# Two mixers of a fused two-block model: recurrence in one pass, squares summed on TensorE, conditioning steps at fixed places

## The chip, the cores and the metric

One core of a Trainium2 chip runs the whole program. The metric is the device time of one execution in microseconds (us). TensorE is written PE, VectorE DVE, ScalarE ACT, GpSimd POOL and SyncE SP, as in the profile.

## What is computed

Two model blocks run one after the other on 256 tokens of width 1024. The change touches the first block alone, which has two layers, and 16 tokens are put ahead of the 256, so that T = 272. A layer is a mixer and a feed-forward part. Cut to the mixer:

```python
hn = rms_norm(h, norm_mix_g[l])
q, k, v, xr, gate = jnp.split(hn @ w_in[l], splits, axis=-1)
o_attn = rms_norm(diff_attention(q, k, v, lam), subln_g[l]) * (1.0 - lam_init)
# recurrent branch: conv of width 4 over xr gives xc; r and i are sigmoids of small products of xc
log_a = LRU_C * r * log_sigmoid(lru_L);  a = exp(log_a)
u = sqrt(max(-expm1(2 * log_a), 0)) * i * xc          # the root is replaced by 1 at token 0
h_t = a_t * h_(t-1) + u_t                             # along the tokens
o_rec = rms_norm(h_t * gelu(gate), rec_norm_g[l])
h = h + concatenate([o_attn, o_rec]) @ w_out[l]       # 512 + 512 rows of w_out
```

Beside this the program computes `silu(c) @ w_ada` (the conditioning), which only the second block reads.

## The kernel before

**Layout.** Activations of the first block are held with channels on partitions: `h` is 8 chunks of 128 channels by 272 tokens. Each fp32 product is three fp32r products (`mm3`, lines 364 to 366): high part of the weight with high and with low part of the input, and low part with high. `weights()` hands out the next weight block, loads run three blocks ahead on SP's queue, and each block is split by ACT (`whi`, line 340) and DVE (`wlo`, line 342).

**A mixer** (`first_mixer`). After the projections for k, q and v, `first_attend` (a generator) does the attention of two tiles of 128 tokens; each of its first four steps is a head, its fifth normalises and transposes the tile's output into `mh` and `ml`, chunks 0 to 3. Between the heads the loop traces `taps(c)` (projection and convolution of chunk c) and `gate(c)` (projection, gelu, the two small products of line 749 and four ACT functions). Then come the root over all four chunks (line 776), `recurrence(c)` for each chunk (lines 758 to 762, scan on 761), the sum of its squares over channels, a reciprocal root per token (`rstd_row` and `rsqrt`, lines 399 to 407, then the broadcast by PE on line 451 and the copy `RR`), and the multiplication and split into `mh` and `ml`, chunks 4 to 7 (lines 783 to 785).

**The output projection** runs in two halves, first over chunks 0 to 3 of `mh` (attention), then over 4 to 7 (recurrence). Each half has four weight blocks b of two output chunks c, 96 products in all. Each result is added to `h` from PSUM (line 799).

**PSUM.** `acc` has 3 banks, `st` 1, and the mixer has `sc` 2, `pt` 1, `po` 1. `pt` is shared by the transposes of the heads and the products of the gates.

**Conditioning.** `ada_steps` is a generator of 32 steps, 16 for each mixer. A step loads a tile of 512 KB (`wada`, five buffers; the first five loads on SP's queue, the others on POOL's) and does four matmuls of 32 columns (line 487, eight passes in the trace) into an `acc` bank that is held over 16 steps. The 16th also copies the bank (line 492) and transposes it (line 496).

**Order.** Within an engine the order is fixed when the program is built: a scheduler takes, of the instructions that it believes to be ready, the one that was traced first. `high_priority` counts a block as traced earlier. `issue_after(x)` makes instructions of a block queue behind x on the engine of x, without a wait. Each engine then takes its instructions strictly in that order.

Of the kernel before, what the change touches and what calls it, by code (L numbers as in the profile page):

```python
# [7 lines left out]
F32 = mybir.dt.float32  # L8
# [24 lines left out]
HP = 400  # L33
ADA = ((4, 4, 4, 2), (4, 4, 4, 0))
SUMS = ((0, 4), (0, 5)) + tuple((1, p) for p in range(6))
# [247 lines left out]
class Net:  # L283
# [83 lines left out]

    def gemm(self, w, m, xs, cols, n, ps=None):

        if ps is None:  # L370
            ps = self.psum("acc")[:, :n]
        m = slice(128 * m, 128 * m + 128)
        for k, (wk, xk) in enumerate(zip(w, xs, strict=True)):
            self.mm3(ps, [t[:, m] for t in wk], [t[:, cols] for t in xk], k == 0, k == len(w) - 1)
        return ps
# [57 lines left out]

    def rstd_row(self, pool, ss, tiles, width, mul, name, eps=EPS, extra=False):


        nc = self.nc
        st = self.psum("st")
        big = [(i, t) for i, t in enumerate(tiles)]
        for i, (t0, tn) in big:  # L440
            a0 = t0 if tn == 128 else 0
            nc.tensor.matmul(st[:, i:i + 1], ss[:, a0:a0 + 128], self.ones[:, 0:1], start=True, stop=True)
        n = len(tiles) + extra
        if extra:
            for j in range(4):
                nc.tensor.matmul(st[32 * j:32 * j + 32, n - 1:n], ss[:, 0:32], self.ones[:, 0:1], start=True, stop=True,
                                 tile_position=(0, 32 * j))
        y, v = self.rsqrt(st[:, :n], (128, n), mul, eps, "ry", pool)
        bc = self.psum("st")
        for i, (t0, tn) in big:  # L450
            nc.tensor.matmul(bc[:, t0:t0 + tn], y[0:tn, i:i + 1].to_broadcast([tn, 128]), self.idt[0:tn, 0:tn],
                             start=True, stop=True)
# [21 lines left out]
    def ada_steps(self):  # L474
# [3 lines left out]
        for b in range(2):  # L478
# [14 lines left out]
            cols = [j for j in range(4) if 4 * b + j not in (4, 5, 10, 11)]  # L493
            p2 = self.psum("st")
            for m in range(4):
# [124 lines left out]
    def first_mixer(self, l, mp, fp):  # L620
# [102 lines left out]

        xc, gts = [], []
        tr = mp.tile([128, 4, T], F32, name="tr")
        th = mp.tile([128, 4, T], F32, name="th")

        def taps(c):
            xr = mp.tile([128, T], F32, tag="xr", name="xr", bufs=2)
            nc.vector.tensor_tensor(xr, self.gemm(self.weights(), 0, xs, al, T), R, op=ALU.mult)  # L730
            x = mp.tile([128, T], F32, name=f"xc{c}")
            cw = self.par("conv_w", l, 0, 16)
            nc.scalar.activation(x, xr, AF.Identity, scale=cw[:, 12 + c:13 + c], bias=self.par("conv_b", l, c))
            for i in range(3):
                s = 3 - i
                nc.vector.scalar_tensor_tensor(x[:, s:], xr[:, :T - s], cw[:, 4 * i + c:4 * i + c + 1], x[:, s:],
                                               op0=ALU.mult, op1=ALU.add)
            xc.append(x)

        def gate(c):  # L740
            x = xc[c]
            gt = mp.tile([128, T], F32, name=f"gt{c}")
# [10 lines left out]
            nc.vector.scalar_tensor_tensor(x, ti, 1.0, x, op0=ALU.add, op1=ALU.mult)  # L753

        rs = mp.tile([128, T], F32, name="rs")

        def recurrence(c):
            nc.vector.scalar_tensor_tensor(th[:, c], tr[:, c], 1.0, th[:, c], op0=ALU.add, op1=ALU.mult)
            nc.vector.memset(th[:, c, 0:1], 1.0)
            nc.vector.tensor_tensor(xc[c], xc[c], th[:, c], op=ALU.mult)  # L760
            nc.vector.tensor_tensor_scan(xc[c], tr[:, c], xc[c], 0.0, op0=ALU.mult, op1=ALU.add)
            nc.vector.tensor_tensor(xc[c], xc[c], gts[c], op=ALU.mult)
            self.sumsq_add(rs, self.sp, xc[c], c == 0, T)

# [5 lines left out]
        for i in range(2):  # L770
            for u, _ in enumerate(att(i)):
                if u < 4:
                    f, c = next(parts)
                    f(c)
        nc.vector.tensor_scalar(th, th, 0.0, None, op0=ALU.max)
        nc.scalar.activation(th, th, AF.Sqrt)
        for c in range(4):
            recurrence(c)
        RR, _, _ = self.rstd_row(mp, rs, tiles, T, 1.0 / (512 * 16), "RR")
        g4 = mp.tile([128, 4], F32, name="g4")  # L780
        nc.vector.tensor_scalar(g4, self.par("rec_norm_g", l, 0, 4), 0.25, None, op0=ALU.mult)
        for c in range(4):
            nc.vector.tensor_tensor(xc[c], xc[c], RR, op=ALU.mult)
            nc.scalar.activation(mh[:, 4 + c], xc[c], AF.Copy, scale=g4[:, c:c + 1])
            nc.vector.scalar_tensor_tensor(ml[:, 4 + c], xc[c], g4[:, c:c + 1], mh[:, 4 + c].bitcast(F32),
                                           op0=ALU.mult, op1=ALU.subtract)


        oc = slice(0, T) if l + 1 < DEPTH else slice(META, T)
        on = oc.stop - oc.start  # L790
        g = self.par("norm_ffn_g", l, 0, 8)
        for half in (0, 1):
            ys = [(mh[:, 4 * half + k], ml[:, 4 * half + k]) for k in range(4)]
            for b in range(4):
                w = self.weights()
                for m in range(2):
                    c = 2 * b + m
                    ps = self.gemm(w, m, ys, oc, on)
                    nc.vector.tensor_tensor(self.h[:, c, oc], self.h[:, c, oc], ps, op=ALU.add)
                    if half == 1:  # L800
                        self.cols = oc
                        self.first_pre(c, g)
                if half == 0:
                    self.ada_step(ADA[l][b])

    def first_attend(self, mp, l, i, qk, vn, aq, nlam, sub, mh, ml):
# [10 lines left out]
        for h in units:  # L817
# [39 lines left out]
            if i < 2:  # L857
                o = po[:, 128 * h:128 * h + 128]
                nc.tensor.matmul(o, am, vn[2][0:16, h], start=True, stop=False)
                for j in range(nt):  # L860
                    nc.tensor.matmul(o, a[:, 128 * j:128 * j + 128], vn[j][:, h], start=False, stop=j == nt - 1)
# [24 lines left out]
        nc.scalar.activation(mh[:, 0:4, d], src, AF.Copy, scale=sub)  # L886
        nc.vector.scalar_tensor_tensor(ml[:, 0:4, d], src, sub, mh[:, 0:4, d].bitcast(F32), op0=ALU.mult, op1=ALU.subtract)
        yield
# [713 lines left out]
```

## Time and profile before

| what | value |
|---|---|
| time, median of 3 runs | 1690.88 us (1690.41 to 1691.0) |
| the profiled execution, its own time | 1690.12 us |
| its span, first to last instruction | 1688.3 us |
| mean granted clock of PE | 0.987 of full speed |
| PE / weight loads / DVE / ACT / POOL busy | 97% / 83% / 75% / 50% / 4% |
| mixer 0 | to about 159 us |
| mixer 1 | about 364 to 513 us |

A line of the timeline has the start, the length, the engine, the line of the kernel, the operation, output<-inputs, the count and, in brackets, the idle time before it and who ended it. PE lengths overlap: matmuls are pipelined, and two starts tell more than one length. A granted clock of 1.00 is 2.4 GHz and 0.50 is 1.2 GHz; a value between them is a mean over both.

### The profile page before, as it was taken

Reading aid. Unit: us, or ns where it says so; the run is one execution under the profiler, and the core shown is the slowest. Engines: PE = TensorE matmul, PEld = TensorE weight load, DVE = VectorE, ACT = ScalarE, POOL = GpSimd, SP = SyncE. Lnnn points to the kernel's source line nnn. Section 1 sums busy time; section 2 is a strip of 40 time slices with the busy share of each in tenths; the row PEclk is TensorE's granted clock in tenths of the full one; section 3 lists DMA queues with packets and bytes.
Section 4 is the critical chain, followed back from the end, with each engine's and each line's share of the span. In section 5 each row is a group of like instructions: output and inputs, shape, how many; then the busy total and the mean of one; then the engine's idle time right before and its main releaser. Section 6 shows DMA issues by size and latency. Waiting matters only on the chain.

```text
span 1688.3 us, 27336 instructions
## 1 busy us (share of the span) xinstructions
PE 1638.9 (97%) x10336; PEld 1397.0 (83%) x10336; DVE 1258.5 (75%) x2706; ACT 846.6 (50%) x1607; POOL 69.5 (4%) x143
## 2 busy tenths in 40 slices
PE   7999999999989999999999999999999999979998
PEld 7868999998869999997667987788787786679997
DVE  7678897675878776664566887898986978587777
ACT  5575544354747544534465543232332757665554
POOL 0001000000010000000010000001110000000000
PEclk9999999999989999999999999999999999989999
DMA  7546665464356656523223254556672231245663
GB/s 260 163 149 240 200 211 174 154 193 149 102 175 192 182 183 188 181 76 100 64 69 111 78 162 137 187 162 200 220 242 87 90 98 40 65 131 184 184 186 112
DMA packets 71852, 256.77 MB, mean 152 GB/s; under 512 B 8585, under 2 KB 8601, under 8 KB 71721
## 3 DMA queue, kind: packets, MB, share of 16 engines
q1 hardware_dynamic: 56904, 203.58, 38.1%
q0 software_dynamic: 14672, 51.45, 9.5%
q8 instruction: 81, 1.33, 0.3%
q14 instruction: 51, 0.41, 0.1%
q10 hardware_dynamic: 144, 0.00, 0.0%
HBM read 253.92 MB, written 1.07 MB: 151 GB/s over the span
## 4 chain that ended last, share of the span: by engine, by line
PE 79%; issue 10%; DVE 5%; ACT 3%; DMA 2%; POOL 0%; DVEq 0%; ACTq 0%; SPq 0%; POOLq 0%
PE acc L364 14%; PE acc L365 14%; PE acc L366 14%; PE up L365 6%; PE up L364 6%; PE up L366 6%; PE y L364 2%; PE y L366 2%; PE y L365 2%; PE po L1390 2%; PE pt L1384 2%; DVE wlo L342 1%; ACT whi L340 1%; PE sc L1379 1%; DMA wada<-wada 1%
## 5 line engine op out<-in xcount | busy, mean ns | idle before, releaser
L340 ACT ACTIVATE whi<-raw 128x1024 fp32r<-128x1024 f32 (+2 forms) x436 | 397.2, 924 | 540.3 <-PE acc L365 245.3
L342 DVE TENSOR_TENSOR wlo<-raw,whi 128x1024 fp32r<-128x1024 f32 (+2 forms) x436 | 456.6, 1055 | 209.5 <-ACT whi L340 204.2
L364 PE MATMUL acc<-hi,whi 128*128 128x272 f32 (+1 forms) x848 | 248.7, 294 | 8.1 <-ACT hi L575 7.4
L366 PE MATMUL acc<-hi,wlo 128*128 128x272 f32 (+1 forms) x848 | 246.4, 291 | 0.8 <-DVE wlo L342 0.8
L365 PE MATMUL acc<-lo,whi 128*128 128x272 f32 (+1 forms) x848 | 246.6, 291 | 0.0
L364 PEld LDWEIGHTS acc<-hi,whi 128*128 128x128 f32 x848 | 161.9, 191 | 15.7 <-ACT hi L575 7.7
L364 PE MATMUL acc<-op,whi 128*128 128x256 f32 (+1 forms) x528 | 165.3, 315 | 0.0
L365 PE MATMUL acc<-op,whi 128*128 128x256 f32 (+1 forms) x528 | 164.1, 312 | 0.1
L366 PE MATMUL acc<-op,wlo 128*128 128x256 f32 (+1 forms) x528 | 163.4, 310 | 0.0
L365 PEld LDWEIGHTS acc<-lo,whi 128*128 128x128 f32 x848 | 161.8, 191 | 1.7 <-DVE lo L576 0.3
L366 PEld LDWEIGHTS acc<-hi,wlo 128*128 128x128 f32 x848 | 161.8, 191 | 1.2 <-DVE wlo L342 0.8
L364 PE MATMUL acc<-whi,op 128*128 128x512 f32 (+1 forms) x424 | 151.1, 357 | 0.1
L365 PE MATMUL acc<-wlo,op 128*128 128x512 f32 (+1 forms) x424 | 150.8, 356 | 0.0
L365 PE MATMUL up<-op,whi 128*128 128x512 f32 (+1 forms) x384 | 146.6, 382 | 0.0
L364 PE MATMUL up<-op,whi 128*128 128x512 f32 (+1 forms) x384 | 145.6, 381 | 0.8 <-ACT whi L340 0.7
L366 PE MATMUL up<-op,wlo 128*128 128x512 f32 (+1 forms) x384 | 145.4, 380 | 0.0
L366 PEld LDWEIGHTS acc<-op,wlo 128*128 128x128 f32 x528 | 100.7, 191 | 7.9 <-issue 3.0
L531 DVE SCALAR_TENSOR_TENSOR asum<-wadb,csp,asum 128x1024 f32<-128x1024 f32 x84 | 107.1, 1276 | 0.0
L364 PEld LDWEIGHTS acc<-op,whi 128*128 128x128 f32 x528 | 99.6, 189 | 7.9 <-issue 1.6
L365 PEld LDWEIGHTS acc<-op,whi 128*128 128x128 f32 x528 | 99.6, 189 | 7.0 <-issue 1.5
L364 PEld LDWEIGHTS acc<-whi,op 128*128 128x128 f32 x424 | 80.0, 189 | 13.2 <-issue 0.7
L365 PEld LDWEIGHTS acc<-wlo,op 128*128 128x128 f32 x424 | 79.8, 188 | 12.8 <-issue 1.8
(443 smaller groups left out, 3380.7 us busy)
## 6 DMA issues: line engine op xcount, KB each, us to landing
raw<-wts SPq DMA_DIRECT2D x362, 512.0 KB, 3.8
wadb<-wadb POOLq DMA_DIRECT2D x64, 512.0 KB, 4.0
wada<-wada POOLq DMA_DIRECT2D x27, 512.0 KB, 6.3
raw<-wts SPq DMA_DIRECT2D x8, 384.0 KB, 3.1
B<-brow SPq DMA_DIRECT2D x6, 512.0 KB
wada<-wada SPq DMA_DIRECT2D x5, 512.0 KB, 6.3
nb<-nbias POOLq DMA_DIRECT2D x16, 128.0 KB, 2.4
h<-xm SPq DMA_DIRECT2D x4, 272.0 KB, 4.1
```

The costliest lines, as they stand in the source:

```text
L340: nc.scalar.activation(hi[:, cs], raw[:, cs], AF.Copy)
L342: nc.vector.tensor_tensor(lo[:, cs], raw[:, cs], hi[:, cs].bitcast(F32), op=ALU.subtract)
L364: mm(out, a[0], b[0], start=start, stop=False)
L365: mm(out, a[0], b[1], start=False, stop=False)
L366: self.product = mm(out, a[1], b[0], start=False, stop=stop)
L531: nc.vector.scalar_tensor_tensor(acc[s], w, c, acc[s], op0=ALU.mult, op1=ALU.add)
L1379: done = mm(ps[i], q[a][rows[i], tok], k[b][rows[i], k0:k0 + nk], start=n == 0, stop=n == 2)
L1384: nc.tensor.transpose(pt[:, 128 * j:128 * j + 128], p[:, 128 * j:128 * j + 128], self.idt)
L1390: mm(po[rows[i]], v[k0 // 128 + j][:, vc:vc + 64], pT[i][j // 2][:, 256 * (j % 2):256 * (j % 2) + 256], start=j == 0, stop=j == nj - 1, ti ...
```

## The change

The recurrence's `xc` becomes one tile of four chunks. Each chunk's `max` is done in its gate, and the addition, the token-0 constant and the multiplication are one DVE instruction each over 1088 columns. The squares of each chunk are no longer added on DVE: PE sums them chunk by chunk into `st` (`recurrence_sums`), and one small DVE reduction adds the four. Chunks 0 and 1 are queued behind the last product of block 1 of half 0, chunk 2 behind that of block 2, chunk 3 behind that of block 3. Output chunks 0 to 3 stay in the banks `sc`, `sc`, `po`, `pt` over both halves. Conditioning steps get fixed places: in mixer 0 one each behind units 2 and 5, in both mixers four behind the last value product of the attention, and two behind each block of half 0. The last step of the attention's second tile is traced later, at high priority, and its `ml` is queued on DVE behind the product over all chunks.

```diff
-ADA = ((4, 4, 4, 2), (4, 4, 4, 0))
+ADA = ({2: 1, 5: 1}, {})
...
-    def gemm(self, w, m, xs, cols, n, ps=None):
+    def gemm(self, w, m, xs, cols, n, ps=None, first=True, last=True):
...
-            self.mm3(ps, [t[:, m] for t in wk], [t[:, cols] for t in xk], k == 0, k == len(w) - 1)
+            self.mm3(ps, [t[:, m] for t in wk], [t[:, cols] for t in xk], first and k == 0, last and k == len(w) - 1)
...
-            p2 = self.psum("st")
+            p2 = self.psum("acc")
...
             nc.vector.scalar_tensor_tensor(x, ti, 1.0, x, op0=ALU.add, op1=ALU.mult)
-
-        rs = mp.tile([128, T], F32, name="rs")
+            nc.vector.tensor_scalar(th[:, c], th[:, c], 0.0, None, op0=ALU.max)
 
         def recurrence(c):
-            nc.vector.scalar_tensor_tensor(th[:, c], tr[:, c], 1.0, th[:, c], op0=ALU.add, op1=ALU.mult)
-            nc.vector.memset(th[:, c, 0:1], 1.0)
-            nc.vector.tensor_tensor(xc[c], xc[c], th[:, c], op=ALU.mult)
-            nc.vector.tensor_tensor_scan(xc[c], tr[:, c], xc[c], 0.0, op0=ALU.mult, op1=ALU.add)
-            nc.vector.tensor_tensor(xc[c], xc[c], gts[c], op=ALU.mult)
-            self.sumsq_add(rs, self.sp, xc[c], c == 0, T)
+            x = xc[:, c]
+            nc.vector.tensor_tensor_scan(x, tr[:, c], x, 0.0, op0=ALU.mult, op1=ALU.add)
+            nc.vector.tensor_tensor(x, x, gts[c], op=ALU.mult)
+            nc.scalar.activation(th[:, c], x, AF.Square)
+
+        def recurrence_sums(st, c):
+            for i, (t0, tn) in enumerate(tiles):
+                a0 = t0 if tn == 128 else 0
+                nc.tensor.matmul(st[:, 4 * i + c:4 * i + c + 1], th[:, c, a0:a0 + 128], self.ones[:, 0:1], start=True,
+                                 stop=True)
...
         for i in range(2):
-            for u, _ in enumerate(att(i)):
-                if u < 4:
-                    f, c = next(parts)
-                    f(c)
-        nc.vector.tensor_scalar(th, th, 0.0, None, op0=ALU.max)
+            tile = att(i)
+            for u in range(4):
+                next(tile)
+                f, c = next(parts)
+                f(c)
+                with self.tc.issue_after(self.product.ins):
+                    self.ada_step(ADA[l].get(4 * i + u, 0))
+            if i == 0:
+                next(tile)
+        with self.tc.issue_after(self.value.ins):
+            self.ada_step(self.ada_bufs - 1)
         nc.scalar.activation(th, th, AF.Sqrt)
+        nc.vector.scalar_tensor_tensor(th, tr, 1.0, th, op0=ALU.add, op1=ALU.mult)
+        nc.vector.memset(th[:, :, 0:1], 1.0)
+        self.inputs = nc.vector.tensor_tensor(xc, xc, th, op=ALU.mult)
+        with self.tc.high_priority(HP):
+            next(tile)
         for c in range(4):
             recurrence(c)
-        RR, _, _ = self.rstd_row(mp, rs, tiles, T, 1.0 / (512 * 16), "RR")
...
+        def normed(st):
+            n = len(tiles)
+            s = self.sp.tile([128, 64], F32, tag="sv", name="sv")[:, :n]
+            nc.vector.tensor_reduce(s, st[:, :4 * n].rearrange("p (i c) -> p i c", c=4), axis=AX.X, op=ALU.add)
+            RR = self.rstd_row(mp, None, tiles, T, 1.0 / (512 * 16), "RR", st=s)[0]
...
+        kept = {}
+        st = self.psum("st")
         for half in (0, 1):
...
-                    ps = self.gemm(w, m, ys, oc, on)
-                    nc.vector.tensor_tensor(self.h[:, c, oc], self.h[:, c, oc], ps, op=ALU.add)
+                    if half == 0 and c < 4:
+                        kept[c] = self.psum(("sc", "sc", "po", "pt")[c])[:, :on]
+                    ps = self.gemm(w, m, ys, oc, on, kept.get(c), half == 0 or c not in kept, half == 1 or c not in kept)
+                    if half == 1 or c not in kept:
+                        nc.vector.tensor_tensor(self.h[:, c, oc], self.h[:, c, oc], ps, op=ALU.add)
...
                 if half == 0:
-                    self.ada_step(ADA[l][b])
+                    with self.tc.issue_after(self.product.ins):
+                        for c in ((), (0, 1), (2,), (3,))[b]:
+                            recurrence_sums(st, c)
+                        self.ada_step(2)
+            if half == 0:
+                normed(st)
...
-        nc.vector.scalar_tensor_tensor(ml[:, 0:4, d], src, sub, mh[:, 0:4, d].bitcast(F32), op0=ALU.mult, op1=ALU.subtract)
+        with self.tc.issue_after(self.inputs.ins) if i == 1 else nullcontext():
+            nc.vector.scalar_tensor_tensor(ml[:, 0:4, d], src, sub, mh[:, 0:4, d].bitcast(F32), op0=ALU.mult,
+                                           op1=ALU.subtract)
```

## Rows read from the trace of the kernel before

**Rows 1.** Page, busy time, share of the span and instructions of each engine.

```profile
PE 1638.9 (97%) x10336; PEld 1397.0 (83%) x10336; DVE 1258.5 (75%) x2706; ACT 846.6 (50%) x1607; POOL 69.5 (4%) x143
```

**Rows 2.** Waits of PE: who, for whom, us in total, times, longest.

```profile
PE acc L487 <- DMA wada<-wada: 7.4, 5, 3.1
```

**Rows 3.** Stretches: length, busy per engine (instructions), granted clock, DMA share, GB/s.

```profile
120.20:124.50 4.30, 1.28 (x18) 0.32 (x17) 3.71 (x17) 2.77 (x5) 2.00 (x4) 0.97 1.00 332
124.50:128.60 4.10, 4.10 (x22) 1.59 (x22) 2.18 (x7) 0.79 (x2) 0.53 (x1) 0.61 0.99 388
...
144.40:146.70 2.30, 1.94 (x22) 1.04 (x20) 2.30 (x6) 2.12 (x4) 0.53 (x1) 1.00 0.41 162
...
477.00:482.40 5.40, 5.40 (x25) 2.42 (x26) 2.52 (x8) 1.12 (x2) 0.00 (x0) 0.50 0.35 143
...
495.60:499.00 3.40, 1.86 (x13) 1.26 (x11) 2.96 (x9) 2.06 (x4) 1.59 (x3) 1.00 0.52 158
499.00:503.10 4.10, 4.10 (x20) 3.95 (x21) 3.67 (x10) 1.27 (x3) 0.00 (x0) 0.59 0.96 322
```

**Rows 4.** Timeline of PE, mixer 0.

```profile
114.45 0.28 PE L849 MATMUL pt<-con,p 128*16 128x128 f32 x1
...
116.39 0.71 PE L861 MATMUL po<-vn,aT 128*128 128x128 f32 x4
...
125.49 1.12 PE L879 MATMUL pt<-con,on 128*128 128x128 f32 x4
...
128.60 0.40 PE L365 MATMUL acc<-ml,whi 128*128 128x272 f32 x1
...
136.97 0.72 PE L442 MATMUL st<-con,rs 128*128 128x1 f32 x6
137.56 0.37 PE L365 MATMUL acc<-ml,whi 128*128 128x272 f32 x1
```

**Rows 5.** Timeline of ACT, mixer 0.

```profile
115.16 0.36 ACT L856 ACTIVATE aT<-pt 128x256 f32<-128x256 f32 x1
...
117.14 0.37 ACT L871 ACTIVATE junk<-po,rr 128x128 f32<-128x128 f32 x1 [1.31 <-PE po L861]
...
120.60 1.28 ACT L776 ACT_TABLE_LOAD   x1
121.89 1.11 ACT L776 ACTIVATE th<-th 128x1088 f32<-128x1088 f32 x1
```

**Rows 6.** Timeline of DVE, mixer 0.

```profile
113.04 0.50 DVE L846 SCALAR_TENSOR_TENSOR p<-p,ra 128x272 f32<-128x272 f32 x1
...
120.61 0.17 DVE L399 TENSOR_SCALAR rv<-so 128x4 f32<-128x4 f32 x1 [0.25 <-ACT junk L871]
...
122.59 0.69 DVE L875 TENSOR_TENSOR on<-po,ro 128x512 f32<-128x512 f32 x1
...
127.36 0.75 DVE L887 SCALAR_TENSOR_TENSOR ml<-pt,subg,mh 128x512 fp32r<-128x512 f32 x1 [1.90 <-ACT mh L886]
...
137.74 0.16 DVE L399 TENSOR_SCALAR rv<-st 128x3 f32<-128x3 f32 x1 [1.05 <-PE st L442]
137.81 1.23 DVE L342 TENSOR_TENSOR wlo<-raw,whi 128x1024 fp32r<-128x1024 f32 x1
...
140.90 0.16 DVE L407 SCALAR_TENSOR_TENSOR ry<-rh,ry 128x3 f32<-128x3 f32 x1
...
143.74 1.32 DVE L785 SCALAR_TENSOR_TENSOR ml<-xc,g,mh 128x272 fp32r<-128x272 f32 x3
```

**Rows 7.** Timelines of mixer 1, PE and DVE.

```profile
468.18 0.71 PE L861 MATMUL po<-vn,aT 128*128 128x128 f32 x4
...
490.50 0.16 DVE L399 TENSOR_SCALAR rv<-st 128x3 f32<-128x3 f32 x1 [0.59 <-PE st L442]
...
495.87 0.14 DVE L407 SCALAR_TENSOR_TENSOR ry<-rh,ry 128x3 f32<-128x3 f32 x1
...
499.53 0.45 PE L365 MATMUL acc<-ml,whi 128*128 128x256 f32 x1
```

More of the change, by code (lines that the diff above doesn't have):

```diff
@@ L432, in sumsq_add, with rstd_row @@
             nc.vector.tensor_tensor(ss, ss, t, op=ALU.add)
-    def rstd_row(self, pool, ss, tiles, width, mul, name, eps=EPS, extra=False):
+    def rstd_row(self, pool, ss, tiles, width, mul, name, eps=EPS, extra=False, st=None):
         nc = self.nc
-        st = self.psum("st")
         big = [(i, t) for i, t in enumerate(tiles)]
-        for i, (t0, tn) in big:
+        summed = st is not None
+        if not summed:
+            st = self.psum("st")
+        for i, (t0, tn) in () if summed else big:
             a0 = t0 if tn == 128 else 0
@@ L721, in first_mixer @@
         nlam = self.neg_lambda(mp, l)
-        xc, gts = [], []
+        xc, gts = mp.tile([128, 4, T], F32, name="xc"), []
         tr = mp.tile([128, 4, T], F32, name="tr")
@@ L730, in taps @@
             nc.vector.tensor_tensor(xr, self.gemm(self.weights(), 0, xs, al, T), R, op=ALU.mult)
-            x = mp.tile([128, T], F32, name=f"xc{c}")
+            x = xc[:, c]
             cw = self.par("conv_w", l, 0, 16)
@@ L737, in taps @@
                                                op0=ALU.mult, op1=ALU.add)
-            xc.append(x)
         def gate(c):
-            x = xc[c]
+            x = xc[:, c]
             gt = mp.tile([128, T], F32, name=f"gt{c}")
@@ L753, in gate @@
             nc.vector.scalar_tensor_tensor(x, ti, 1.0, x, op0=ALU.add, op1=ALU.mult)
-        rs = mp.tile([128, T], F32, name="rs")
+            nc.vector.tensor_scalar(th[:, c], th[:, c], 0.0, None, op0=ALU.max)
         def recurrence(c):
-            nc.vector.scalar_tensor_tensor(th[:, c], tr[:, c], 1.0, th[:, c], op0=ALU.add, op1=ALU.mult)
-            nc.vector.memset(th[:, c, 0:1], 1.0)
-            nc.vector.tensor_tensor(xc[c], xc[c], th[:, c], op=ALU.mult)
-            nc.vector.tensor_tensor_scan(xc[c], tr[:, c], xc[c], 0.0, op0=ALU.mult, op1=ALU.add)
-            nc.vector.tensor_tensor(xc[c], xc[c], gts[c], op=ALU.mult)
-            self.sumsq_add(rs, self.sp, xc[c], c == 0, T)
+            x = xc[:, c]
+            nc.vector.tensor_tensor_scan(x, tr[:, c], x, 0.0, op0=ALU.mult, op1=ALU.add)
[6 more added lines that the diff above has]
+                                 stop=True)
         att = lambda i: self.first_attend(mp, l, i, qk, vn, aq, nlam, sub, mh, ml)
@@ L780, in first_mixer @@
         g4 = mp.tile([128, 4], F32, name="g4")
         nc.vector.tensor_scalar(g4, self.par("rec_norm_g", l, 0, 4), 0.25, None, op0=ALU.mult)
[L782 to L786, printed above, removed]
+        def normed(st):
[3 more added lines that the diff above has]
+            RR = self.rstd_row(mp, None, tiles, T, 1.0 / (512 * 16), "RR", st=s)[0]
+            for c in range(4):
+                x = xc[:, c]
+                nc.vector.tensor_tensor(x, x, RR, op=ALU.mult)
+                nc.scalar.activation(mh[:, 4 + c], x, AF.Copy, scale=g4[:, c:c + 1])
+                nc.vector.scalar_tensor_tensor(ml[:, 4 + c], x, g4[:, c:c + 1], mh[:, 4 + c].bitcast(F32),
+                                               op0=ALU.mult, op1=ALU.subtract)
@@ L791, in first_mixer @@
         g = self.par("norm_ffn_g", l, 0, 8)
+        kept = {}
+        st = self.psum("st")
         for half in (0, 1):
@@ L860, in first_attend @@
                 for j in range(nt):
-                    nc.tensor.matmul(o, a[:, 128 * j:128 * j + 128], vn[j][:, h], start=False, stop=j == nt - 1)
+                    self.value = nc.tensor.matmul(o, a[:, 128 * j:128 * j + 128], vn[j][:, h], start=False, stop=j == nt - 1)
             else:
```

## Prediction

> **What bounds the kernel now.** I read the engine shares first: TensorE (PE) is busy for 97% of the span [rows 1], so time can only come from the stretches where PE idles or runs at half clock, and any work put on PE has to be paid for. The list of what PE waited for shows where the first kind lies in this change's reach: conditioning products (line 487) that wait for their own weight transfers [rows 2]. I then cut the two mixers of the first block into stretches by the granted clock [rows 3] and read them in the timelines: PE [rows 4], ACT [rows 5] and DVE [rows 6] of mixer 0, and the same places of mixer 1 [rows 7]. Outside 60 to 165 us and 440 to 515 us nothing is touched, and I take those parts as unchanged.
>
> In each mixer I look at three stretches. *The gap*: from the last input projection (111.6 and 463.7 us) to a steady stream of output products. *Half 0* of the output projection. *The seam* between half 0 and half 1, whose inputs are the normalised recurrence. In mixer 0 the gap ends at 128.60, the first product with `ml` [rows 4]. Until then PE has run ten conditioning steps and been starved by their transfers: 1.28 us busy of 4.30, then a granted clock of 0.61, that is largely the 1.2 GHz level [rows 3]. `on` was ready at 123.3 [rows 6], but its transposes stood behind those products until 125.49 [rows 4]. Mixer 1 is the same but worse, at 0.50 until 482.4 [rows 3]. The seam is 2.3 us long in mixer 0, all at full clock and filled with conditioning and transposes; in mixer 1 PE is busy for 1.86 of 3.40 us there and then runs at a mean clock of 0.59 for 4.1 us [rows 3].
>
> **Unit prices.** One conditioning step is 8 passes, about 0.53 us of PE at full clock. A pass of a sum of squares, with one output column, is 0.098 us: six passes from 136.97 to 137.56 [rows 4]. A fall of the clock costs the length times what was missing: 4.1 x (1 - 0.59) = 1.7 us at 499.0, 4.1 x 0.39 = 1.6 us at 124.5, 5.4 x 0.50 = 2.7 us at 477.0 [rows 3]; I take 1.7, measured on a stream of output products, with 0 and 2.7 as the ends. A chain of nine tiny DVE instructions (the reciprocal root) is 1.8 us undisturbed: ten of them lie between 120.61 and 122.59 [rows 6].
>
> **The gap.** Held back are the conditioning steps: four may run after the last value product, the others sit behind fixed products. Two more go into the attention units of mixer 0, where PE has no room, so everything behind them moves by 1.06 us (0 if the softmax chain and not PE is what is late there; the end I do not take). In exchange the last head is no longer blocked: its probabilities were ready at 113.54 [rows 6] but transposed at 114.45 [rows 4], and its `aT` was ready at 115.5 [rows 5] but used at 116.39 [rows 4]; 1.8 us in mixer 0, some 0.8 us in mixer 1 by the same reading. So the value products end at 117.10 - 1.8 + 1.06 = 116.4 and at 468.89 - 0.8 = 468.1 [rows 4, 7].
> From there a serial chain runs that the change keeps and extends: 3.5 us of ACT work (squares of the attention output, the last gate) from 117.14 to the table load at 120.60, 1.3 us of table load, 1.1 us of square root over 1088 columns [rows 5]. Then come the two DVE passes over all chunks at once, 1088 columns each: a pass over 1024 takes 1.23 us with its overlap [rows 6], so 1.2 each, 2.4 together. `ml` is now queued behind them, 0.7 us [rows 6], and the second product of every accumulation needs `ml`. Together 9.0 us: steady products from 125.4 and 477.1, against 128.6 and 482.4 now. That is -3.2 us and, since 0.3 us of products had been done before 482.4, -5.0 us. `on`, its transposes and `mh` lie beside the root and the two passes, and so do the four conditioning steps, whose tiles are all there: with five buffers filled long before, nothing is starved. What is late next is the root chain, not the transfer. PE idles in more than half of those 9 us, so I let the clock fall here in both mixers: +1.7 each at the start of half 0 (mixer 1 pays 2.7 now, but before 482.4, which is inside the -5.0).
>
> **Half 0.** Six conditioning steps now lie ahead of its last product. It holds 18 passes (2.25 steps) in mixer 0 and two steps in mixer 1 now, so +2.0 and +2.1 us. The squares go through PE chunk by chunk, 24 passes per mixer instead of 6: 12 more in half 0 (+1.2 us), 6 in the seam. In mixer 0 the broadcast of the reciprocal root (line 451, 1.0 us) leaves half 0 for the seam: -1.0. Sum +2.2 and +3.3. The Trainium skill ("TensorE: Matmul & The Clock Gate", section on the back-to-back issue gap) gives a product of 1 to 64 columns a floor of about 25 ns; by that the 36 added passes of both mixers would cost 0.9 instead of 3.5 us and the sum would be some 2.6 us lower. The row has 98 ns, each pass with a new stationary tile, and the row decides.
> Entered at nothing: the four sums that stay in PSUM take four DVE additions from each half 0, but DVE is beside PE there and PE hardly waits for them; the banks `sc`, `po` and `pt` are free by then (`pt` when `ml` is written, which PE waits for anyway); the conditioning's transposes move to an `acc` bank that is free because half 1 starts in kept banks. If `acc` were short, that would cost a wait of one eviction, below 0.5 us. The loads of the moved steps stay on POOL's queue (the first five on SP's), each waiting for its buffer only; on POOL nothing but further conditioning loads stands behind them before half 1, on SP three of the five move among weight loads that are three blocks ahead.
>
> **The seam.** This is what decides. The squares of the fourth chunk may be summed only behind the last product of half 0, because they are queued behind it by hand, though they are ready some 10 us sooner. Half 1 cannot start without them. From there: 0.8 us from the first summing pass to the first tiny DVE instruction (136.97 to 137.74), 0.2 us for the new reduction, 1.8 us of root, and from its end at 141.06 to the end of the first new `ml` at 144.2 the broadcast, the copy of `RR`, the multiplications and the split: 3.1 us [rows 4, 6]. 5.9 us if nothing comes between. Now the root chain is disturbed both times: 137.74 to 141.06 in mixer 0 with a weight split of 1.23 us in it [rows 6], 490.50 to 496.0 in mixer 1 [rows 7], 1.5 and 3.7 us more than undisturbed. So the bounds are 5.9 and 9.6 us; fewer additions compete now, one weight block becomes free exactly there, so I take one split: 7.0 us in both. PE has 0.6 us of sums, two conditioning steps, the broadcast and (mixer 0) transposes to do in it, some 3.2 us; the rest is idle.
> Mixer 0: 7.0 instead of 2.3, +4.7. Mixer 1: from 495.6 the steady product comes at 499.53 now [rows 3, 7], 3.9 us; +3.1. The clock: in mixer 0 it stays up today and I let it fall, +1.7; in mixer 1 it falls already, 0.
>
> **Sum.** Mixer 0: -3.2 + 1.7 + 2.2 + 4.7 + 1.7 = +7.1. Mixer 1: -5.0 + 1.7 + 3.3 + 3.1 = +3.1. Together +10.2 us on the profiled execution's 1690.12 us (span 1688.3 us and 1.8 around it; the median of the runs is 1690.88, 0.8 above): 1700.3 us, 0.6% slower.
>
> **Rivals.**
> *The seam keeps its clock and its chain is undisturbed.* For: the seam of mixer 0 stays at 1.00 today with conditioning in it [rows 3]. Against: in mixer 1 the clock was lost though PE idled for 1.54 us of 3.40 in all [rows 3]. Price: -1.1 in each seam, -1.7 in mixer 0's clock, -1.7 in mixer 1's that it pays today: -5.6, so 1694.7 us. Beside it: the Trainium skill (same page, section on why this matters) warns of long idle gaps between bursts; by that rule so little idle time would leave the clock up, and this rival would be the forecast. The row at 495.6 speaks against the rule, so it has a chance of 0.15.
> *Nothing to see.* As above, and the steady stream starts 2 to 3 us sooner in each gap because the last gate's ACT work runs while the last head's values are still on PE, so that the 3.5 us are not in series: some 1690 us. For: ACT idles in pieces before 117.14. Against: gate and head share the one `pt` bank, which is what the chain waited for. Chance 0.15.
> *The other side: faster.* The starved conditioning is what cost the gap; held back, it keeps PE supplied through the gap in small portions. If the clock never falls in the gap (-3.4) and `mh` and `ml` of the attention come 3 us before my estimate (-6.0) while the seam goes as in the first rival (-5.6), the sum is 1690.1 + 10.2 - 15.0 = 1685.3 us. It decides if steady products start before about 122.5 and 474.2. For: 7.4 us of transfer waits go away for certain [rows 2]. Against: the table load, root and two passes are serial and `ml` stands behind them. Chance 0.12.
> *Worse.* The root chain is cut into as it is in mixer 1 now, 9.6 us in both seams (+5.2), or a fixed conditioning step waits for its transfer on PE: 1705.5 us. Chance 0.13.
> That the edges do not hold what they name can be left out: they are plain queue order.
>
> **How the numbers follow.** Forecast 0.45: 1700.3 us, from 1696 to 1704 by the ends of clock and chain. The range leaves out the faster rival and about half of the one without a difference: 1690 to 1707. A measurement of this kernel can tell about 0.2% (3.4 us) from no change. Slower by more than that: forecast, first rival and worse, 0.45 + 0.15 + 0.13 = 0.73; within it 0.15; faster 0.12.
>
> **What the profile after would show.** PE's wait for `wada` transfers near nothing. The first steady output product some 9 us behind the last value product, and `ml` right behind the product over 1088 columns on DVE. Four groups of sums of six passes, the last one behind the last product of half 0, and then 6 to 8 us to the first product of half 1 in both mixers, with a low clock behind it. I am wrong if half 1 follows half 0 within 3 to 4 us, or if the gap ends before 123 us in mixer 0. If the time is lower and the seam as long as I say, the gap is what I misjudged.

## The result

The changed kernel takes 1708.55 us (median; 1708.05 to 1710.22), the kernel before beside it 1690.73 us (1690.41 to 1691.0): 17.8 us or 1.1% slower, ratio 1.0114 with a 95% interval of 1.0102 to 1.0126. The forecast was 1700.3 us. The sign was right; the loss was 7.6 us larger than the working made it, and just outside the range. Its profiled execution has a span of 1706.5 us (1688.3 before).

The views of the changed kernel, in the same order as before. The first line of the page, and from the list of what PE waited for (us in total, times, longest):

```profile
PE 1646.0 (96%) x10372; PEld 1405.7 (82%) x10372; DVE 1254.9 (74%) x2682; ACT 847.6 (50%) x1607; POOL 69.5 (4%) x143
...
PE st L453 <- DVE ry L407: 4.0, 3, 2.3
...
PE sc L364 <- ACT mh L917: 3.6, 2, 2.3
PE sc L365 <- DVE ml L919: 3.4, 2, 2.0
PE sc L364 <- ACT mh L805: 3.0, 2, 1.5
PE pt L910 <- DVE on L906: 1.9, 2, 1.6
PE pt L880 <- DVE p L877: 1.7, 1, 1.7
```

PE's waits for `wada` transfers [rows 2] are gone, as forecast. In their place stand waits for the split of the attention (L917, L919), for the reciprocal root (L407), for the split of the recurrence (L805) and for the last head (L877). In the kernel before none of these waits came to more than 0.7 us in all.

*The gap of mixer 0* [rows 4 to 6]: PE's timeline, then ACT's and DVE's.

```profile
117.91 1.22 PE L892 MATMUL po<-vn,aT 128*128 128x128 f32 x4
...
119.97 3.62 PE L489 MATMUL acc<-wada,cs 128*32 128x256 f32 x26
123.52 0.89 PE L750 MATMUL pt<-xc,gates 128*128 128x272 f32 x2
...
127.98 0.82 PE L364 MATMUL sc<-mh,whi 128*128 128x272 f32 x2 [2.34 <-ACT mh L917]
...
130.86 0.60 PE L365 MATMUL sc<-ml,whi 128*128 128x272 f32 x1 [1.37 <-DVE ml L919]
```

```profile
124.45 0.49 ACT L751 ACTIVATE ti<-pt,bh 128x272 f32<-128x272 f32 x1 [2.10 <-PE pt L750]
124.95 1.28 ACT L786 ACT_TABLE_LOAD   x1
126.25 1.11 ACT L786 ACTIVATE th<-th 128x1088 f32<-128x1088 f32 x1
```

```profile
127.39 1.29 DVE L787 SCALAR_TENSOR_TENSOR th<-tr,th 128x1088 f32<-128x1088 f32 x1 [1.98 <-ACT th L786]
...
128.85 1.29 DVE L789 TENSOR_TENSOR xc<-xc,th 128x1088 f32<-128x1088 f32 x1
130.06 0.75 DVE L919 SCALAR_TENSOR_TENSOR ml<-pt,subg,mh 128x512 fp32r<-128x512 f32 x1
```

The four conditioning steps (L489) stand in PE's order ahead of the last gate's second product (L750 at 123.52). They run at 1.2 GHz (clock 0.59 from 119 to 125 us, below), so 26 of their 32 passes take 3.55 us, to 123.52. ACT idles 2.10 us for that product; only then come table load, root, the two passes, and `ml`. Mixer 1 shows the same, with 1.65 us of idle time on ACT (PE's timeline, then ACT's row):

```profile
479.70 2.75 PE L489 MATMUL acc<-wada,cs 128*32 128x256 f32 x24
482.38 0.73 PE L750 MATMUL pt<-xc,gates 128*128 128x272 f32 x2
...
490.06 0.58 PE L365 MATMUL sc<-ml,whi 128*128 128x256 f32 x1 [2.02 <-DVE ml L919]
```

```profile
483.15 0.49 ACT L751 ACTIVATE ti<-pt,bh 128x272 f32<-128x272 f32 x1 [1.65 <-PE pt L750]
```

*The seam of mixer 0*: PE's timeline, then DVE's.

```profile
149.26 0.72 PE L766 MATMUL st<-con,th 128*128 128x1 f32 x6
149.91 1.07 PE L489 MATMUL acc<-wada,cs 128*32 128x256 f32 x16
151.70 0.66 PE L498 MATMUL acc<-con,apart 128*128 128x128 f32 x4 [0.72 <-ACT apart L494]
153.99 1.22 PE L453 MATMUL st<-con,ry 128*128 128x128 f32 x6 [1.63 <-DVE ry L407]
156.72 0.82 PE L364 MATMUL sc<-mh,whi 128*128 128x272 f32 x2 [1.51 <-ACT mh L805]
...
158.03 0.43 PE L365 MATMUL sc<-ml,whi 128*128 128x272 f32 x1
```

```profile
150.22 0.17 DVE L399 TENSOR_SCALAR rv<-sv 128x3 f32<-128x3 f32 x1
...
150.51 1.22 DVE L342 TENSOR_TENSOR wlo<-raw,whi 128x1024 fp32r<-128x1024 f32 x1
...
152.39 0.38 DVE L502 TENSOR_TENSOR ada<-acc,par 128x8 f32<-128x8 f32 x4 [0.59 <-PE acc L498]
...
153.68 0.16 DVE L407 SCALAR_TENSOR_TENSOR ry<-rh,ry 128x3 f32<-128x3 f32 x1
```

The fourth sums start at 149.26, right behind half 0, and the first product with `ml` of half 1 comes at 158.03, 8.8 us later: PE idles 0.72 + 1.63 + 1.51 = 3.9 us of it. The root chain takes 3.6 us (150.22 to 153.84), cut by a weight split and by the additions of the conditioning, ahead of which DVE also idles 0.59 us for PE's transposes. In mixer 1 the two ends lie at 508.85 and 517.96, 9.1 us, and the root chain takes 4.2 us.

The granted clock in stretches of both mixers (busy time of PE, weight loads, DVE, ACT, POOL; the value behind them is PE's clock):

```profile
119.00:125.00 6.00, 5.98 (x38) 2.24 (x37) 2.48 (x13) 3.64 (x13) 1.58 (x3) 0.59 0.54 189
125.00:131.00 6.00, 2.29 (x10) 1.73 (x10) 3.92 (x6) 2.92 (x3) 0.53 (x1) 0.69 0.64 227
131.00:134.00 3.00, 3.00 (x14) 3.00 (x15) 3.00 (x7) 0.78 (x2) 0.00 (x0) 0.50 0.00 0
...
157.00:161.00 4.00, 4.00 (x19) 4.00 (x20) 1.91 (x5) 1.02 (x3) 1.20 (x3) 0.50 1.02 393
...
491.00:494.00 3.00, 3.00 (x16) 3.00 (x15) 2.87 (x7) 1.21 (x3) 0.00 (x0) 0.50 0.00 0
```

Behind both gaps and both seams the products start at 1.2 GHz, half of the full 2.4 (the seam of mixer 1: 0.69 on average from 518 to 521 us). In mixer 0 the clock is at that level before the gap's steps begin, too: it is 0.50 from 117.2 to 123 us.

### The profile page after: what moved, and what is told of

Read it like the earlier page. It is cut to its first block, busy times and chain, and to the rows that moved or that the text cites. A ratio compares the mean times of both kernels' runs of the same rounds, so it can differ in the third digit from the quotient of the medians.

```text
span 1706.5 us, 27379 instructions
## 1 busy us (share of the span) xinstructions
PE 1646.0 (96%) x10372; PEld 1405.7 (82%) x10372; DVE 1254.9 (74%) x2682; ACT 847.6 (50%) x1607; POOL 69.5 (4%) x143
## 4 chain that ended last, share of the span: by engine, by line
PE 88%; DVE 6%; ACT 4%; issue 1%; DMA 0%; DVEq 0%; ACTq 0%; POOLq 0%
PE acc L364 16%; PE acc L365 16%; PE acc L366 16%; PE up L365 6%; PE up L364 6%; PE up L366 6%; PE y L364 2%; PE y L366 2%; PE y L365 2%; PE po L1423 2%; PE pt L1417 2%; DVE wlo L342 1%; PE acc L489 1%; PE sc L1412 1%; ACT whi L340 1%
```

## The experiments

Every kernel was timed beside the kernel before on the same chip, and the verdicts are ratios to it; 0.1% is 1.7 us. The intervals are some ±2 us (95%), so a difference of two ratios is known to about 3 us. A trace is that of one execution; where two traces are compared, the text says from what start. Names that begin with e start from the changed kernel (+19.3 us by its ratio), with b from the kernel before; c are combinations.

### Parts taken back in the changed kernel

**e1_sums_early.**

```diff
-                        for c in ((), (0, 1), (2,), (3,))[b]:
+                        for c in (0, 1, 2, 3) if b == 1 else ():
                             recurrence_sums(st, c)
...
-            if half == 0:
-                normed(st)
+                    if b == 1:
+                        normed(st)
```

> Edit: all four chunks' sums of squares are queued behind the last product of block 1 of half 0, and the reduction, root and broadcast follow from there instead of behind block 3. Theory (the seam is lost to the fixed place of the fourth sums): the root chain runs beside blocks 2 and 3, half 1 follows half 0 within 1.5 to 2.5 us instead of 8.7 and 9.1 us, and the half clock behind the seam of mixer 0 goes (1.0 us); -13 to -15 us, about 1695 us (1692 to 1698). Rival 1 (the seam is set by what half 1 needs besides, its weight split on DVE and the inputs' splits): the seam shortens by less than half, about 1702 us. Rival 2 (the loss sits in the start of half 0, and time won in the seam is waited for again further on): 1706 us or more.

Ratio 1.0061 (1.0044 to 1.0079): +10.3 us, 9.0 less than the changed kernel. PE's timeline at the old place of the seam:

```profile
145.89 1.00 PE L453 MATMUL st<-con,ry 128*128 128x128 f32 x6
...
151.75 1.07 PE L489 MATMUL acc<-wada,cs 128*32 128x256 f32 x16
152.75 0.39 PE L364 MATMUL sc<-mh,whi 128*128 128x272 f32 x1
```

No wait is left; the clock is 1.00 from 147 to 158. The mechanism holds, but my figure was too large: sums, broadcast, transposes and two steps have to be done by PE wherever they stand. What comes back is the idle time and the clock, in mixer 0 3.9 + 1.0 = 4.9 us, and by the first product of the next part (269.95 to 265.31, from a start 0.3 us later) it is 4.9 us.

**e2_cond_behind_gate.**

```diff
-                nc.tensor.matmul(ps[:, :T], gates[:, c, j], x, start=True, stop=True)
+                self.gated = nc.tensor.matmul(ps[:, :T], gates[:, c, j], x, start=True, stop=True)
...
-        with self.tc.issue_after(self.value.ins):
+        with self.tc.issue_after(self.gated.ins):
             self.ada_step(self.ada_bufs - 1)
```

> Edit: the four conditioning steps that were queued behind the last value product are queued behind the second product of the last gate, so ACT gets that gate before the steps run. Theory (these steps hold up the chain of last gate, table load, root, two passes, ml): ACT's wait for that product (2.10 and 1.65 us) goes to some 0.3 us, the steady products start 1.5 to 2 us sooner in each mixer, -3 to -4 us, about 1705 us (1704 to 1706). Rival (PE must do the steps before the transposes anyway and the low clock is what counts): no change, 1708.5 us within 0.8.

Ratio 1.0090 (1.0075 to 1.0105): 4.1 us less than the changed kernel. ACT's row:

```profile
122.81 0.49 ACT L751 ACTIVATE ti<-pt,bh 128x272 f32<-128x272 f32 x1 [0.72 <-PE pt L750]
```

2.10 us of waiting became 0.72, and the first product with `ml` came 1.5 us sooner than in the changed kernel, counted from the last value product. The clock had fallen in this execution as well: ACT's wait in mixer 1 is 0.72 us too (1.65 in the changed kernel).

**e3_ml_free.**

```diff
-        with self.tc.issue_after(self.inputs.ins) if i == 1 else nullcontext():
+        with nullcontext():
             nc.vector.scalar_tensor_tensor(ml[:, 0:4, d], ...
```

> Edit: ml of the attention is no longer queued behind the multiplication over 1088 columns on DVE. Theory: ml comes one pass of 1.2 us sooner in each mixer, the recurrence 0.7 us later, which costs nothing because its squares wait 12 us for their sums; -2 to -2.5 us, about 1706.3 us (1705.5 to 1707). Rival (the later recurrence moves the sums and the seam): no change or up to 1 us slower, 1708.5 to 1709.5 us.

Ratio 1.0082 (1.0067 to 1.0097): 5.4 us less, twice the -2 to -2.5 that one pass per mixer makes. `ml` now stands between the two passes; PE's wait for it falls from 1.37 and 2.02 us to 0.51 and 0.56. Where the rest comes from is not shown; it is within the uncertainty of 3 us.

**e4_no_keep.**

```diff
-                    if half == 0 and c < 4:
+                    if False:
                         kept[c] = ...
```

> Edit: output chunks 0 to 3 of half 0 are added to h and their banks freed, as before the change; all else stays. Theory (the kept banks cost and bring nothing, as the prediction entered them): 1708.5 us within 1.5. Rival (kept banks let five first products per half start ahead of ml, and spare DVE eight additions per mixer in half 0 while it has the recurrence): 2 to 4 us slower, 1710.5 to 1712.5 us. Other rival (keeping them is part of the loss): faster by 2 us or more.

Ratio 1.0114 (1.0099 to 1.0129), the same as the changed kernel: no worth of the kept half shows either way, as entered.

Its trace shows something else. In mixer 1 the four conditioning steps stand ahead of the last gate's second product as in the changed kernel, but the clock there is 1.00 (479 to 483 us). PE's timeline and ACT's row:

```profile
481.20 1.50 PE L489 MATMUL acc<-wada,cs 128*32 128x256 f32 x24
```

```profile
483.54 0.49 ACT L751 ACTIVATE ti<-pt,bh 128x272 f32<-128x272 f32 x1 [0.17 <-PE pt L750]
```

The 24 passes take 1.58 us instead of 2.68, ACT waits 0.17 us instead of 1.65, and the first product with `ml` comes 9.65 us behind the last value product instead of 11.1. Mixer 1 of e1 and of e6 has the same order, the same full clock and the same 0.17 and 9.65 us; mixer 0 of e1, at 0.50, and of e6, at 0.58 on average during the steps, has 2.20 and 1.45 us of waiting. So these steps hold up the last gate where the clock has fallen before them, and not by their place alone.

**e5_cond_as_before** (the steps back in half 0, `ADA = ((4, 4, 4, 2), (4, 4, 4, 0))`, no `issue_after` for them).

> The changed kernel with its conditioning steps placed as before the change (traced in half 0, free to run when the scheduler thinks them ready); recurrence, sums, kept banks and ml stay. Theory (the steps belong where PE idles; the seam is the larger loss and stays): about 14 us above before instead of 18, 12 to 16. Rival 1 (the placement of the steps is the main loss): less than 9 us above. Rival 2 (the steps starve again and stand in front of the transposes, and the later ml adds to it): 18 to 22 us above.

Ratio 1.0046 (1.0029 to 1.0063): +7.8 us, 11.5 less than the changed kernel, and so Rival 1. PE's timeline in the gap, and its windows:

```profile
116.86 1.50 PE L489 MATMUL acc<-wada,cs 128*32 128x256 f32 x24
118.44 0.72 PE L750 MATMUL pt<-xc,gates 128*128 128x272 f32 x2
119.10 0.62 PE L489 MATMUL acc<-wada,cs 128*32 128x256 f32 x4
120.68 0.64 PE L489 MATMUL acc<-wada,cs 128*32 128x256 f32 x8 [0.96 <-DMA wada<-wada]
```

```profile
121.00:127.00 6.00, 4.57 (x49) 1.86 (x41) 4.41 (x7) 2.30 (x3) 1.59 (x3) 1.00 0.99 388
127.00:131.00 4.00, 4.00 (x34) 3.88 (x31) 2.93 (x7) 2.13 (x4) 0.00 (x0) 1.00 0.60 221
```

The starved steps are back, and with them PE is busy for 4.57 of 6.00 us in the gap and keeps its full clock; `ml` is used at 127.13 instead of 130.86 (its start was 0.4 us earlier). The 24 passes ahead of the last gate's second product take 1.58 us here, at full clock.

**e6_no_unit** (the two steps in the attention units of mixer 0 stand in block 0 of half 0).

> The changed kernel without the two conditioning steps in the attention units of mixer 0; both stand in block 0 of half 0 of that mixer instead. Theory (there they upset the order of scores and projections and cost 3.5 us, far over their 1.06 us of work): the last value product of mixer 0 ends 3.5 us sooner, half 0 is 1.06 us longer, -2.5 us in all (-1.5 to -3). Rival (each step costs its 0.53 us wherever it stands): no change, within 0.5 us.

Ratio 1.0087 (1.0073 to 1.0100): 4.6 us less, where -1.5 to -3 was expected. The last head's transposes:

```profile
112.71 0.27 PE L880 MATMUL pt<-con,p 128*16 128x128 f32 x1
```

They stand at 116.35 in the changed kernel, behind a wait of 1.68 us. From a start 0.8 us earlier, the last value product ends 3.5 us sooner (119.13 to 114.87). Two steps, 1.06 us of work, put the scores of that head off (their second half starts at 108.84 instead of 105.94) and with them the whole softmax. By the first product of the next part (269.95 to 266.88, 0.8 us of it the start) mixer 0 is 2.3 us shorter, as expected; the rest of the 4.6 lies outside it and within the uncertainty.

### Combinations

**c1_three**: e1, e2 and e3 together.

> Edits 1 to 3 together: all sums behind block 1 and the root from there, the four conditioning steps behind the last gate's second product, ml free of the pass over 1088 columns. Apart they gave 9.0, 4.1 and 5.4 us by the ratios to before. Theory: they lie in different places or one behind the other in one serial chain, so they add to 18.5 us and the kernel comes out level with the one before, from 1 us below to 2 us above. Rival (2 and 3 shorten the same wait, mh comes last then): 3 to 5 us less gain, 3 to 5 us above before.

Ratio 1.0014 (1.0003 to 1.0024): +2.4 us, 17 of the expected 18.5 us back. They add, within the uncertainty.

**c2_one_sum**: c1, and the squares added on DVE as before the change.

```diff
-            nc.scalar.activation(th[:, c], x, AF.Square)
+            self.sumsq_add(th[:, 0], self.sp, x, c == 0, T)
...
-            for i, (t0, tn) in enumerate(tiles):
+            for i, (t0, tn) in enumerate(tiles) if c == 0 else ():
...
```

> Like the three edits together, and the squares of the four chunks are added on DVE again as before the change, so PE sums 6 passes per mixer instead of 24. Theory: 18 passes of 0.11 us per mixer were on PE's path, -4.0 us against the three edits together (-3 to -4.5), so 3 to 5 us below before. Rival (the three additions on DVE delay the sums behind block 1 or the weight splits): no gain or up to 1 us slower.

Ratio 0.9984 (0.9975 to 0.9993): 5.1 us less than c1; 36 passes at 0.11 us (24 of them take 2.66 us in e1) make 4.0.

**c3_gap_step**: c2 without steps in the units; one step of each mixer behind the transposes of the attention output, and one more of mixer 0 in block 0 of half 0.

> Like the one before, and no conditioning step in the attention units of mixer 0: one step of each mixer stands behind the transposes of the attention output, where PE idles (0.8 us and more), and one more of mixer 0 in block 0 of half 0. Theory (PE has no room in the units, and idles behind the transposes): -0.5 us in each mixer, -1 us together (0 to -1.5). Rival (steps in the units hide beside the softmax chain): +0.5 us in mixer 0 and -0.5 in mixer 1, no change.

Ratio 0.9966 (0.9954 to 0.9979): -5.7 us, 3.0 less than c2, more than the 0 to -1.5 that I expected, for the reason that e6 shows: the last value product of mixer 0 ends 3.7 us sooner than in c2. PE's timeline of its gap and a window:

```profile
118.70 2.84 PE L489 MATMUL acc<-wada,cs 128*32 128x256 f32 x32
...
122.06 0.64 PE L489 MATMUL acc<-wada,cs 128*32 128x256 f32 x8
122.91 0.52 PE L364 MATMUL sc<-mh,whi 128*128 128x272 f32 x2 [0.21 <-ACT mh L917]
...
124.26 0.39 PE L365 MATMUL sc<-ml,whi 128*128 128x272 f32 x1 [0.45 <-DVE th L788]
```

```profile
125.00:131.00 6.00, 6.00 (x61) 5.09 (x60) 5.97 (x11) 2.14 (x4) 1.57 (x3) 1.00 0.87 307
```

**e7_cond_before_early**: e5 and e1 together. **c4_best**: that, squares on DVE and `ml` free.

> Conditioning as before the change, and all sums of squares behind block 1 with the root from there; recurrence in one pass, sums on PE chunk by chunk, kept banks and the late ml stay. Theory (the seam costs its idle time and clock whatever the conditioning does, and the two losses add): -8 to -9 us against conditioning as before alone, so level with the kernel before, from 2 us below to 1.5 us above it. Rival (conditioning as before fills the seam or delays the sums behind block 1): 3 to 6 us above before.

> Like that one, and the squares added on DVE as before (6 summing passes of PE per mixer) and ml free of the long pass. What is left of the change is the recurrence in one pass, the kept banks and the root beside half 0. Theory: -4 us for 36 passes and -1 to -3 us for ml: 5 to 8 us below before. Rival (ml is no longer what comes last once the starved steps are back): 4 us below before.

Ratios 0.9985 (0.9976 to 0.9994) and 0.9966 (0.9953 to 0.9979): -2.5 and -5.7 us, the first just below its expected range and the second inside. c3 and c4 beat both kernels by the same amount: fixed places are not bad in themselves, if the steps stand where PE idles.

### Parts alone in the kernel before

**b1_cond_alone**: the new places of the conditioning steps alone. **b2_late_sums**: the six sums of squares behind the last product of half 0, root and split from there. **b3_places_late**: both. In all three the conditioning's transposes go to an `acc` bank, as in the change.

> The kernel before with the new places of the conditioning steps alone. Theory (of the changed kernel's loss some 11 us are the places: steps in the units, steps ahead of the last gate, eight steps instead of two in half 0): 8 to 12 us above before. Rival (the places hurt only together with the serial chain over all chunks and the late sums): 0 to 4 us above before.

> The kernel before with one edit: the six sums of the recurrence's squares stand behind the last product of half 0, and root, broadcast and split follow from there. Conditioning, recurrence and banks stay as they were. Theory (the seam costs its idle time and its clock whatever else is done): about 3.9 us idle and 1 us of clock in mixer 0, some 4 us in mixer 1, 7 to 10 us above before. Rival (the freely placed conditioning fills the seam): 2 to 4 us above before.

> The kernel before with the new places of the conditioning steps and the late sums of squares together; recurrence chunk by chunk, squares added on DVE, ml free, banks as they were. The places alone gave +3.6 us. Theory (the places cost more once the seam is late too, because then nothing in the half hides the steps that the seam used to hold): 13 to 15 us above before, and the rest of the loss, some 5 us, is the 36 more passes and the late ml. Rival (places and late sums only add): the sum of +3.6 and what the late sums give alone, 10 to 12 us; then 7 us or more are left for the passes and the late ml.

Ratios 1.0021 (1.0010 to 1.0033), 1.0054 (1.0037 to 1.0071) and 1.0072 (1.0059 to 1.0085): +3.6, +9.1 and +12.2 us. The places alone cost far less than the 8 to 12 us expected. Places and late sums add (12.7), which was the rival of the last text. The seam of b2 shows the waits of the changed kernel, with the conditioning free:

```profile
148.72 1.00 PE L453 MATMUL st<-con,ry 128*128 128x128 f32 x6 [1.63 <-DVE ry L407]
151.23 1.05 PE L364 MATMUL acc<-mh,whi 128*128 128x272 f32 x3 [1.52 <-ACT mh L787]
```

But the places cost 3.6 us here and 11.5 in the changed kernel. What they meet there was tried next.

**b4_one_pass**: the recurrence in one pass alone. **b5_one_pass_late_ml**: that, and `ml` behind the long multiplication, with the last step of the tile traced later at high priority as in the change. **b6_pass_places** and **b7_pass_places_late_ml**: the same two with the new places.

> The kernel before with the recurrence in one pass alone (one tile for the four chunks, max in each gate, the addition, the constant of token 0 and the multiplication once over 1088 columns); conditioning, sums on DVE and PE, and ml as they were. Theory (this part helps a little, by taking nine instructions from DVE in the gap): 1 to 4 us below before. Rival (it does nothing that the end sees): within 1 us.

> Like that, and ml of the attention queued behind the multiplication over 1088 columns as in the change. Theory (in the changed kernel this was worth 5 us, because the products stand in PE's order behind ml): 2 to 5 us above the run with the one pass alone. Rival (with the conditioning where it was, PE has work until ml comes): within 1 us of it.

> The kernel before with the recurrence in one pass and the new places of the conditioning steps; ml free, sums and root as they were. One pass alone gave -1.9 us, the places alone +3.6. Theory (ml free: the two only add): +1 to +3 us against before. Rival (the one pass itself is what the fixed places do not bear): +6 us or more.

> Like that, with ml queued behind the long multiplication. One pass and late ml with free conditioning gave -3.9 us. Theory (late ml costs only when no free conditioning step is left to fill the wait for it): +6 to +8 us against before, 4 to 6 us above the run with ml free. Rival (places and late ml add): -0.3 us against before, and level with the run with ml free.

Ratios 0.9989 (0.9981 to 0.9998), 0.9977 (0.9967 to 0.9987), 1.0000 (0.9991 to 1.0009) and 1.0020 (1.0008 to 1.0032): -1.9, -3.9, 0.0 and +3.4 us. b4 lies in its expected range and b6 just below; b5 was expected 2 to 5 us above b4. With free steps the late `ml` costs nothing (-2.0), with fixed ones 3.4 us. What stands ahead of the first product with `ml` differs, in b5 and in b7:

```profile
130.68 1.82 PE L487 MATMUL acc<-wada,cs 128*32 128x256 f32 x16
132.44 0.40 PE L365 MATMUL acc<-ml,whi 128*128 128x272 f32 x1
```

```profile
129.05 0.60 PE L365 MATMUL acc<-ml,whi 128*128 128x272 f32 x1 [2.35 <-DVE ml L898]
```

Free, two steps run while `ml` is being made; fixed, PE waits 2.35 us and the steps come later. That this wait makes the 3.4 us is argued and not shown: the execution of b7 that was profiled took 1689.02 us, 5 us below the median of its runs. The direction is shown, the size (5.4 us between the two pairs) only to about 3 us, and b7 lies below the +6 to +8 I expected. Along this side the parts add up to 3.4 (b7) + 8.6 (late sums, b3 less b1) + 5.1 (passes, c1 less c2) = 17 us, against 17.8 to 19.3 measured.

## Why the prediction was right, and where it was not

The sign, the empty list of transfer waits and the worth of kept banks came out as written. The seam is the largest term of the loss, as forecast (11.7 of 17.8 us below), though taking back the places of the steps won at least as much (11.5 us in e5, 9.0 in e1). By its own terms (us, before to after, mixer 1 counted from its own arrival, 10.6 us late):

| term | mixer 0 forecast | measured | mixer 1 forecast | measured |
|---|---|---|---|---|
| start of half 0 (first product with `ml`) | -3.2 | +2.3 | -5.0 | -2.3 |
| half 0 with the clock at its start | +3.9 | +2.6 | +5.0 | +4.9 |
| seam | +4.7 | +6.5 | +3.1 | +5.2 |
| half 1 (clock behind the seam) | +1.7 | +1.0 | 0 | -0.6 |
| sum | +7.1 | +12.4 | +3.1 | +7.2 |

Between the mixers 1.8 us of it are won back, so the terms make 12.4 - 1.8 + 7.2 = 17.8 us, 7.6 above the forecast's 10.2. Two terms came out too low, the gap by 8.2 and the seam by 3.9 us; half 0, half 1 and the part between came out 4.5 us better than forecast.

*The gap* (8.2 us) failed in two steps. First, "two more go into the attention units ..., so everything behind them moves by 1.06 us": e6 shows 3.5 us. I priced the work and not the place; the steps came ahead of scores that a whole softmax chain waits for. (Without them, in e6, the head ends 1.2 us sooner than before, counted from an equal start; I had credited 1.8.)

Second, I let the clock fall only at the start of half 0 and put the four conditioning steps beside the chain, at nothing. The clock fell earlier, after PE had waited 1.68 and 0.35 us for the last head in mixer 0: the steps ran at 1.2 GHz, 26 passes in 3.55 us and 24 in 2.68, and ACT waited 2.10 and 1.65 us for the gate product behind them. So the chain of 9.0 us took 11.7 and 11.1 us. At full clock it takes 9.65 us with the same order (mixer 1 of e1, e4 and e6), so there the steps do lie beside it, and the working was nearly right. How much of this a kernel pays differs between executions and is in part luck; putting the steps behind the gate product, as in e2, made ACT's wait 0.72 us even at 1.2 GHz. In all, PE worked at 0.50 for 29 us of the two mixers in the changed kernel's profile and for 12 us in the profile before; how much of the other losses is clock stays open. The rest of the chain was right: load and root 2.4 us as forecast, the two passes 2.7 for 2.4, `ml` 0.75 for 0.7.

*The seam* (3.9 us) went as described, and one size was off: 8.8 and 9.1 us for 7.0. The root chain took 3.6 and 4.2 us (1.8 undisturbed, 2.9 with the one split that I allowed): the additions of the last conditioning step (L502) cut in as well, because those steps now end there. Five first products run in the seam at half clock, ahead of the first one with `ml`; they account for 1.3 us. The end of 9.6 us that I kept for the rival "worse" was nearer than the value I took, and the measured 1708.55 us lies beyond that rival's 1705.5.

The rival with a kept clock in the seam is refuted by the row at 157.00. The Trainium skill ("TensorE: Matmul & The Clock Gate", section on a second failure mode) tells of short idle times between groups of products that let the clock swing between its levels; the seam, with waits of 0.72, 1.63 and 1.51 us and one fall to 0.50, agrees with that section.

And one thing that the sum had no term for: an order that is free also fills waits that were not there when it was written. The prediction credited the fixed places with ending the starved products. By b1, the places cost 3.6 us on balance in the kernel before; in the changed kernel, where `ml` comes late, nothing is left to fill the wait.

## What to carry to other kernels

Work that an engine can do at any time belongs where the engine idles, and moving it is priced by who stands behind it in that engine's order, not by its length: two steps of 0.53 us cost 3.5 us ahead of a softmax chain, and four of them in front of one small product cost ACT 0.17 us of waiting at 2.4 GHz and up to 2.10 at 1.2. A reduction whose inputs are ready early should be queued early, so that its serial chain runs beside other work; queued at the end of a stage it shows in full, 9.1 us for two mixers when done alone. Price each part of such a change alone and with the others: the late `ml` was free by itself and cost some 3 to 5 us beside the fixed steps. And read the clock of a stretch before a wait in it is put down to the order of the work.

## What the runs showed of the hardware

In the changed kernel PE waited 1.68 and 0.35 us for the last head of mixer 0; the clock was 1.00 from 115 to 116.3 us and 0.50 from 117.2 to 123, and it stayed down while PE worked almost without a break (5.98 of 6.00 us from 119 to 125, mean clock 0.59). The gap behind that, with PE busy for 2.29 of 6.00 us, had a mean of 0.69 and was followed by 3 us of uninterrupted products at 0.50. The gap of e5, with PE busy for 4.57 of 6.00 us, kept 1.00, and so did the products behind it. In mixer 1 of the changed kernel the clock fell while PE waited for `ml` (0.51 from 489.1 to 490.06) and was still 0.50 from 491 to 494, when PE no longer waited.

The same instructions in the same order met a different clock in different runs: 24 conditioning passes took 2.68 us at 0.52 in mixer 1 of the changed kernel and 1.58 us at 1.00 in that of e4. A pass with one output column and a new stationary tile costs 0.11 us also in a row of 24 (2.66 us in e1); the six of the kernel before took 0.098 us each.
